# A decoder block on one core: the product of the convolution's two halves moves behind the low part of a later pair's second weights

## The chip, the cores and the metric

The kernel runs on one core of a Trainium2 chip. The metric is the time of one execution on the device in microseconds (us), as the median of several runs. The core has five engines that work side by side, each through an instruction queue of its own in the order in which the program was written out for it: TensorE (PE; its loading of weights is shown as PEld), VectorE (DVE), ScalarE (ACT), GpSimd (POOL) and SyncE (SP), which here only issues DMAs. An engine waits for another one at semaphores.

## The reference, cut to what matters

One decoder layer on 1024 positions of width 1024: gated linear attention and sparse attention side by side, then a gated feed-forward part with a short convolution, then a gated extra input, each followed by a layer norm. All is float32. The part that the change touches is this one, with `w_up` of 1024 x 5632 and `w_down` of 2816 x 1024:

```python
h = causal_dwconv(x @ w_up[i], conv_w[i], conv_b[i])
h_gate, h_val = jnp.split(h, 2, axis=-1)
ffn = (jax.nn.silu(h_gate) * h_val) @ w_down[i]
```

`causal_dwconv` gives each of the 5632 columns three weights over positions: `out[t] = w[2]*h[t] + w[1]*h[t-1] + w[0]*h[t-2] + b`.

## The kernel before, in words

**Products in parts.** TensorE multiplies in float32r. Each float32 operand is split into a high part (a cast, `hi_of`, L101) and a low part, what the cast lost (a subtraction, `lo_of`, L106), and a product is three matmuls: high by high, high by low, low by high (`mm3`). In the up stage the high part is cast on ScalarE ("wh" in the profile, written from the raw weights "wr" or "ar") and the low part ("wl") is made on GpSimd.

**Seven products for eight.** The up product x @ w_up goes through Strassen's scheme in Winograd's form. A column pair f (`up(f)`, 22 of them) is one block of 128 gate columns and one of 128 value columns. Its weights are four quarters of two raw tiles; four sums on VectorE (`left_operands`, the sums through L164, in place) make from them the seven left operands W0 to W6. In the order of the code: W0, first sum (a11 - a21), W5, second sum (a21 + a22, the profile's "ar<-ar" or "wr<-wr" with one input tile named), third sum (a22 - a11), W1, W2, W3, W4, fourth sum (a12 - a22), W6. A sum that overwrites a quarter has to wait until the parts made of it have been read: the fourth sum waits for W4's low part. The seven products p0 to p6 are 12 matmuls of 128x512 each, 84 for a pair, into PSUM banks "ch".

**From the products to the activation.** The results are added to two tiles "h" (value half and gate half, 128x1024) by VectorE (`plus`, L1043, one input a PSUM bank) and ScalarE (L1050 behind p0, L1074 behind p4). `conv(i)` then scales a half by the third convolution weight and adds the bias on ScalarE (L1085), adds the two shifted terms on VectorE (L1087, two instructions of 128x1023 and 128x1022, both inputs in SBUF), and, for the gate half, takes Silu on ScalarE (L1089), all in a tile "cv". In the stage's steady part `conv(1)` is the value half and `conv(0)` the gate half. GpSimd multiplies the two halves (L164 POOL, "cv<-cv,cv", L1096 calls it), and SP stores the product into `d_act` (L1097), from which the down stage reads it. "cv" has three buffers: the value half's tile is freed by the product, the gate half's by the store.

**What sets the order.** The code of pair f writes out W of pair f, then p0, p1, the late p6 of pair f-1, p5, `conv0` of f-1 (with the product and the store), p2, p3, p4 and `conv1` (the loop `for f in range(NF)`). A scheduler with a timeline of its own then reorders each engine's instructions before the program is built, so that the order on an engine isn't that of the code; an edge set by `tc.issue_after(x)` makes the instructions of a block come after x on x's engine. What each engine does in which order is fixed in the program.

Of the kernel before, what the change touches and what calls it, by code (L numbers as in the profile page):

```python
# [40 lines left out]
def hybrid_block(ctx: ExitStack, tc: tile.TileContext, x, p, w_in, w_gate_up, b_gate, g_gla, w_gla,  # L41
                 g_ckv, w_uv, w_dsa, w_out, ln1_g, ln1_b, w_up, conv_w, conv_b, w_down, ln2_g, ln2_b,
                 w_ple, w_ple_gate, ln3_g, ln3_b, out, tap=None):
    nc = tc.nc
    V, S, G, T = nc.vector, nc.scalar, nc.gpsimd, nc.tensor
# [9 lines left out]
    def pool(name, bufs=1, space=bass.MemoryType.SB, stack=ctx, **kw):  # L55
        return stack.enter_context(tc.tile_pool(name=name, bufs=bufs, space=space, reuse_waits="tile", **kw))
# [9 lines left out]
    def psum_banks(stack, tag, **kw):  # L66
        for name, bufs in kw.items():
            PS[name] = pool(f"ps_{tag}_{name}", bufs, PSUM, stack)
# [21 lines left out]
    def nm(s):  # L90
        uid[0] += 1
        return f"{s}_{uid[0]}"

    def bank(kind="mm", shape=(P, HALF)):
        return PS[kind].tile(list(shape), F32, name=nm(kind), tag=kind)

    done = {}

    def hi_of(dst, src, eng, scale=1.0):
        if eng == "A":  # L100
            S.activation(dst, src, AF.Copy, scale=scale)  # L101
        else:
            (V if eng == "V" else G).tensor_scalar(dst, src, scale, 0.0, ALU.mult, ALU.add)  # L103

    def lo_of(dst, src, hi, eng):
        done["GV"[eng != "G"]] = (G if eng == "G" else V).tensor_tensor(out=dst, in0=src, in1=hi.bitcast(F32), op=ALU.subtract)  # L106

    def split(hi, lo, src, eh="A", el="V"):
        hi_of(hi, src, eh)
        lo_of(lo, src, hi, el)  # L110
# [46 lines left out]
    def mm3(ps, l, r, start, stop, more=False):  # L157

        mm(ps, l[0], r[0], start, False, more)
        mm(ps, l[0], r[1], False, False, more)  # L160
        mm(ps, l[1], r[0], False, stop, more)

    def sums(out, a, b, op, eng="V"):
        (G if eng == "G" else V).tensor_tensor(out=out, in0=a, in1=b, op=op)  # L164

    def left_operands(a11, a12, a21, a22, put, e="VVVV"):

        return [lambda: put(0, a11),
                lambda: sums(a11, a11, a21, ALU.subtract, e[0]),
                lambda: put(5, a22),
                lambda: sums(a21, a21, a22, ALU.add, e[1]),
                lambda: sums(a22, a22, a11, ALU.subtract, e[2]),
                lambda: put(1, a22),
                lambda: put(2, a21),
                lambda: put(3, a11),
                lambda: put(4, a12),
                lambda: sums(a12, a12, a22, ALU.subtract, e[3]),  # L180
                lambda: put(6, a12)]
# [33 lines left out]
    def quad(a):  # L215
        return a.rearrange("p (a b) -> p a b", b=P)
# [39 lines left out]
    def run(steps):  # L256
        for f in steps:
            f()
# [16 lines left out]
    d_act = [dp.tile([P, 6, L], F32, name=f"d_act{c}") for c in range(4)]  # L275
# [47 lines left out]
    with ExitStack() as mix:  # L323
# [65 lines left out]
        with ExitStack() as c1:  # L389
# [95 lines left out]
            raw = wp.tile([P, 1024], F32, name=nm("wr"), tag="wr", bufs=2)  # L485
# [512 lines left out]
    with ExitStack() as c1:  # L998
        psum_banks(c1, "d", ch=8)
        fp = pool("ffwork", stack=c1)  # L1000
        rawp = pool("raws", stack=segd, side="right")
        wk = pool("upwork", stack=segk, side="right")
        UE, UE0, US = 'GGGGGGG', 'VVGVVGV', 'VVVV'
        nset = [0]

        def blocks(f):

            return (NF + f, f) if f < NF - 1 else (f, NF + f)

        def w_sets(f):  # L1010
            raw = []
            for c in blocks(f):
                if f % 2:
                    raw.append(rawp.tile([P, 6, 256], F32, name=nm("ar"), tag="ar", bufs=3)
                               .rearrange("p a b -> p (a b)")[:, :1024])
                else:
                    raw.append(wp.tile([P, 1024], F32, name=nm("wr"), tag="wr", bufs=2))
                nc.sync.dma_start(raw[-1].rearrange("p (k c) -> p k c", k=KT), wup_v[:, :, c * P:(c + 1) * P])
            W = []
            for _ in range(7):  # L1020
                n = nset[0] % 7
                nset[0] += 1
                pl, nb = (wq, 4) if n < 4 else (fp, 3)
                W.append([pl.tile([P, 512], F32R, name=nm(x), tag=x, bufs=nb) for x in ("wh", "wl")])
            run(left_operands(raw[1][:, :512], raw[1][:, 512:], raw[0][:, :512], raw[0][:, 512:],
                              lambda j, src: split(*W[j], src, "A", (UE if f else UE0)[j]), US))
            return [[quad(t) for t in w] for w in W]

        def up(f):

            W = w_sets(f)
            st, out_ = {}, {}

            def prod(ps, j, start):
                for k in range(4):
                    mm3(ps, (W[j][0][:, k], W[j][1][:, k]), (XS[j][:, 0, k], XS[j][:, 1, k]), start and k == 0, k == 3,
                        not start)  # L1040

            def plus(out, a, b):
                V.tensor_tensor(out=out, in0=a, in1=quad(b), op=ALU.add)  # L1043

            def p0():
                st["A"] = bank("ch")
                prod(st["A"], 0, True)
                st["h"] = [wk.tile([P, L], F32, name=nm("h"), tag=f"h{i}", bufs=2) for i in range(2)]
                st["hv"] = [h.rearrange("p (a g q) -> p g a q", g=2, q=P) for h in st["h"]]
                S.activation(st["hv"][1][:, 0], quad(st["A"]), AF.Copy)  # L1050

            def p1():
                st["B"] = bank("ch")
                prod(st["B"], 1, True)
                plus(st["hv"][0][:, 1], st["hv"][1][:, 0], st["B"])

            def p5():
                st["C"] = bank("ch")
                prod(st["C"], 5, True)

            def p2():
                st["D"] = bank("ch")
                prod(st["D"], 2, True)

            def p3():
                prod(st["B"], 3, False)
                s1, u3 = st["hv"][1][:, 0], st["hv"][1][:, 1]
                plus(u3, s1, st["B"])
                plus(s1, u3, st["C"])
                plus(u3, u3, st["D"])  # L1070

            def p4():
                prod(st["A"], 4, False)
                S.activation(st["hv"][0][:, 0], quad(st["A"]), AF.Copy)  # L1074

            def p6():
                prod(st["D"], 6, False)
                o = st["hv"][0][:, 1]
                plus(o, o, st["D"])

            def conv(i):
                c = blocks(f)[1 - i]
                h = st["h"][i]
                o = out_[c // NF] = wk.tile([P, L], F32, name=nm("cv"), tag="cv", bufs=3)
                S.activation(o, h, AF.Identity, bias=cbias[:, c:c + 1], scale=cw[:, 2, c:c + 1])  # L1085
                for d in (1, 2):
                    V.scalar_tensor_tensor(o[:, d:], h[:, :L - d], cw[:, 2 - d, c:c + 1], o[:, d:], ALU.mult, ALU.add)  # L1087
                if c < NF:
                    S.activation(o, o, AF.Silu)  # L1089

            def conv1():
                conv(1)

            def conv0():
                conv(0)
                sums(out_[0], out_[0], out_[1], ALU.mult, "G")  # L1096
                nc.sync.dma_start(d_act[f // 6][:, f % 6], out_[0])  # L1097
            return p0, p1, p5, p2, p3, p4, conv1, p6, conv0

        late = []  # L1100
        for f in range(NF):
            p0, p1, p5, p2, p3, p4, conv1, *rest = up(f)
            run([p0, p1, *late[:1], p5, *late[1:], p2, p3, p4, conv1])
            late = rest
        late[0]()
        last_conv = late[1]
    segx.close()
    sega.close()

# [7 lines left out]
    with ExitStack() as c1:  # L1117
# [88 lines left out]
            merge(*([wd_sets(c, cb)] if gi == 0 else []), *([act_sets(c, gi)] if cb == 0 else []))  # L1206
        prepare(*todo[0])
        with tc.issue_after(done["V"].ins):
            last_conv()
        segk.close()  # L1210
        open_residual(d_x1, 1, "right")
        res_all = RS["pool"].tile([P, NT, D], F32, name="res_all")
# [156 lines left out]
```

## Time and profile before

| | us |
|---|---|
| median of 3 runs | 2147.39 (2147.14 to 2148.36) |
| the profiled execution | 2145.27 |
| its span, first to last instruction | 2143.6 |
| between the two | 1.67 |

In the profile's rows the start is in us from the span's start, then come the duration, the engine, the line of the kernel, the operation, the tile written and the tiles read, and how many instructions are merged in the row (x4). What stands in brackets is how long the engine sat idle before it, and what ended that. The up stage lies between about 1305 and 1740 us; the down stage's first products follow.

### The profile page before, as it was taken

What the parts mean: (1) busy time and instruction counts of PE and PEld (TensorE: products, weight loads), DVE (VectorE), ACT (ScalarE), POOL (GpSimd) and SP (SyncE); (2) the same over time, 40 slices, a digit from 0 to 9 for tenths busy, and PEclk for the clock granted to TensorE, in tenths of its full rate; (3) what the DMA queues carried; (4) which work ended last, traced back from release to release, by engine and by line L of the source; (5) the groups of instructions that cost most, each with busy time, mean ns of one, the idle gap of its engine ahead of it and who ended that gap; (6) DMA issues with size and microseconds to landing.
All of it is one profiled execution on the core that took longest, in us unless ns stands there. A gap on an engine that the chain in (4) does not pass through costs nothing.

```text
span 2143.6 us, 32563 instructions
## 1 busy us (share of the span) xinstructions
PE 2063.3 (96%) x12210; PEld 1811.3 (84%) x12210; DVE 1564.6 (73%) x2742; ACT 846.0 (39%) x1540; POOL 1000.0 (47%) x832
## 2 busy tenths in 40 slices
PE   9999999999999999999999978999999979999997
PEld 8888899998988888887788976877777769989897
DVE  3589999999227888876234487777777788895965
ACT  4343312213126766675222244344344353342421
POOL 2423444535422121213231586776776684554753
PEclk9999999999999999999999998999999989999999
DMA  4322211211226686779766442222222134323222
GB/s 138 79 64 79 86 31 57 57 50 52 64 86 130 130 157 130 144 158 212 205 216 122 147 153 87 86 72 87 81 69 89 64 109 148 118 94 119 89 99 79
DMA packets 377566, 227.14 MB, mean 106 GB/s; under 512 B 189328, under 2 KB 351760, under 8 KB 377408
## 3 DMA queue, kind: packets, MB, share of 16 engines
q1 hardware_dynamic: 377408, 225.06, 38.7%
q8 instruction: 96, 1.57, 0.3%
q14 instruction: 62, 0.51, 0.1%
HBM read 146.37 MB, written 40.89 MB: 87 GB/s over the span
## 4 chain that ended last, share of the span: by engine, by line
PE 29%; DVE 9%; POOL 7%; issue 5%; DMA 3%; ACT 2%; SPq 0%; POOLq 0%; DVEq 0%; ACTq 0%
PE ch L155 16%; PE mm L155 13%; POOL wl L106 4%; DVE cv L1087 1%; DMA wr<-d_ob 1%; DVE cx L164 1%; DMA dr<-in_w_down_dram 1%; DVE h L1043 1%; ACT cv L1085 1%; DVE ar L164 1%; DVE wu L106 1%; DVE res_all L910 1%; DVE res_all L164 0%; DVE stats L933 0%; POOL lnmv L212 0%
## 5 line engine op out<-in xcount | busy, mean ns | idle before, releaser
L106 POOL TENSOR_TENSOR wl<-wr,wh 128x512 fp32r<-128x512 f32 x304 | 439.8, 1461 | 288.3 <-ACT wh L101 280.7
L155 PE MATMUL ch<-xs,wh 128*128 128x512 f32 x1232 | 384.8, 394 | 5.8 <-ACT wh L101 3.2
L155 PE MATMUL mm<-Ah,wh 128*128 128x512 f32 x832 | 332.1, 399 | 2.7 <-ACT wh L101 1.6
L155 PE MATMUL mm<-Al,wh 128*128 128x512 f32 x832 | 330.4, 397 | 0.3 <-POOL Al L106 0.3
L155 PE MATMUL mm<-Ah,wl 128*128 128x512 f32 x832 | 329.4, 396 | 0.0
L155 PEld LDWEIGHTS ch<-xs,wh 128*128 128x128 f32 x1232 | 231.5, 189 | 58.7 <-DVE h L1043 4.1
L103 POOL TENSOR_SCALAR wh<-wr 128x512 fp32r<-128x512 f32 x112 | 75.2, 674 | 381.1 <-PE mm L155 194.4
L155 PE MATMUL ch<-xs,wl 128*128 128x512 f32 x616 | 242.8, 395 | 6.8 <-POOL wl L106 6.7
L155 PE MATMUL mm<-wl,Ah 128*128 128x256 f32 x768 | 217.1, 284 | 5.2 <-POOL wl L106 5.1
L155 PE MATMUL mm<-wh,Al 128*128 128x256 f32 x768 | 215.8, 283 | 0.0
L155 PE MATMUL ch<-wu,au 128*128 128x256 f32 x1512 | 194.0, 292 | 22.5 <-DVE au L106 7.2
L155 PE MATMUL mm<-wh,Ah 128*128 128x256 f32 x768 | 213.2, 283 | 0.0
L1087 DVE SCALAR_TENSOR_TENSOR cv<-h,cw,cv 128x1023 f32<-128x1023 f32 x88 | 168.6, 1915 | 60.0 <-ACT cv L1085 58.5
L155 PEld LDWEIGHTS ch<-wu,au 128*128 128x128 f32 x1512 | 190.4, 199 | 25.9 <-DVE au L106 8.1
L101 ACT ACTIVATE wh<-wr 128x512 fp32r<-128x512 f32 (+1 forms) x201 | 120.5, 623 | 194.7 <-PE mm L155 81.6
L155 PEld LDWEIGHTS mm<-Ah,wh 128*128 128x128 f32 x832 | 156.7, 188 | 33.4 <-ACT wh L101 2.1
L155 PEld LDWEIGHTS mm<-Ah,wl 128*128 128x128 f32 x832 | 156.4, 188 | 33.0
L155 PEld LDWEIGHTS mm<-Al,wh 128*128 128x128 f32 x832 | 156.5, 188 | 30.7 <-POOL Al L106 0.8
L674 DVE MATCH_REPLACE8 score<-m,score 128x896 f32<-128x896 f32 (+3 forms) x192 | 166.5, 869 | 0.0
L673 DVE MAX8 m<-score 128x8 f32<-128x896 f32 (+3 forms) x192 | 163.6, 876 | 2.3 <-POOL score L480 2.1
L155 PEld LDWEIGHTS mm<-wl,Ah 128*128 128x128 f32 x768 | 145.1, 189 | 7.1 <-POOL wl L106 6.4
L155 PEld LDWEIGHTS ch<-xs,wl 128*128 128x128 f32 x616 | 116.5, 189 | 38.2 <-POOL wl L106 14.0
(269 smaller groups left out, 4328.4 us busy)
## 6 DMA issues: line engine op xcount, KB each, us to landing
wr<-in_w_in_dram SPq DMA_DIRECT2D x60, 512.0 KB, 3.8
wr<-in_w_up_dram SPq DMA_DIRECT2D x22, 512.0 KB, 3.9
ar<-in_w_up_dram SPq DMA_DIRECT2D x22, 512.0 KB, 4.0
d_act<-cv SPq DMA_DIRECT2D x22, 512.0 KB, 2.6
dr<-in_w_down_dram SPq DMA_DIRECT2D x12, 768.0 KB, 7.0
ar<-d_act SPq DMA_DIRECT2D x12, 768.0 KB, 5.1
d_tg<-tg SPq DMA_DIRECT2D x32, 256.0 KB, 2.0
wr<-in_w_out_dram SPq DMA_DIRECT2D x16, 512.0 KB, 3.6
```

The costliest lines, as they stand in the source:

```text
L101: S.activation(dst, src, AF.Copy, scale=scale)
L103: (V if eng == "V" else G).tensor_scalar(dst, src, scale, 0.0, ALU.mult, ALU.add)
L106: done["GV"[eng != "G"]] = (G if eng == "G" else V).tensor_tensor(out=dst, in0=src, in1=hi.bitcast(F32), op=ALU.subtract)
L155: T.matmul(ps, lhsT=l, rhs=r, start=start, stop=stop, skip_group_check=more)
L164: (G if eng == "G" else V).tensor_tensor(out=out, in0=a, in1=b, op=op)
L673: V.max(m8, score[t])
L674: V.match_replace(score[t], m8, score[t], TAKEN)
L910: V.scalar_tensor_tensor(r[:, a:b], r[:, a:b], mv[:, 2:3], gb[1][:, a:b], ALU.mult, ALU.add)
L1043: V.tensor_tensor(out=out, in0=a, in1=quad(b), op=ALU.add)
L1085: S.activation(o, h, AF.Identity, bias=cbias[:, c:c + 1], scale=cw[:, 2, c:c + 1])
L1087: V.scalar_tensor_tensor(o[:, d:], h[:, :L - d], cw[:, 2 - d, c:c + 1], o[:, d:], ALU.mult, ALU.add)
```

## The change

The product and its store leave `conv0` and become a step of their own, `store`. Pair f - 2's store is written out in turn f, after the weights of pair f, and has to come after the instruction that `done["G"]` held when W1 of pair f was split, which is W1's low part on GpSimd (for f > 1). The last two stores follow the loop and `last_conv`.

```diff
-            run(left_operands(raw[1][:, :512], raw[1][:, 512:], raw[0][:, :512], raw[0][:, 512:],
-                              lambda j, src: split(*W[j], src, "A", (UE if f else UE0)[j]), US))
+            def put(j, src):
+                split(*W[j], src, "A", (UE if f else UE0)[j])
+                if j == 1 and f:
+                    second[0] = done["G"]
+            run(left_operands(raw[1][:, :512], raw[1][:, 512:], raw[0][:, :512], raw[0][:, 512:], put, US))
...
             def conv0():
                 conv(0)
+
+            def store():
                 sums(out_[0], out_[0], out_[1], ALU.mult, "G")
-                nc.sync.dma_start(d_act[f // 6][:, f % 6], out_[0])
-            return p0, p1, p5, p2, p3, p4, conv1, p6, conv0
-
-        late = []
+                sent[0] = nc.sync.dma_start(d_act[f // 6][:, f % 6], out_[0])
+            return p0, p1, p5, p2, p3, p4, conv1, p6, conv0, store
+
+        late, stores, sent = [], [], [None]
         for f in range(NF):
-            p0, p1, p5, p2, p3, p4, conv1, *rest = up(f)
+            p0, p1, p5, p2, p3, p4, conv1, *rest, store = up(f)
+            if f > 1:
+                with tc.issue_after(second[0].ins):
+                    stores.pop(0)()
+            stores.append(store)
             run([p0, p1, *late[:1], p5, *late[1:], p2, p3, p4, conv1])
             late = rest
+        stores[0]()
         late[0]()
-        last_conv = late[1]
+        last_conv = [late[1], stores[1]]
...
-            last_conv()
+            run(last_conv)
```

What the scheduler made of it differs on three engines; ScalarE's and SP's orders are the same as before. The pair shown is the thirteenth (f = 12); tile numbers differ by two or so between the programs. On GpSimd, before, in the middle of the up stage: these are the low parts of W0 of pair 12, W6 of pair 11 and W5 of pair 12, the product of pair 10, and the low parts of W1, W2 and W3 of pair 12.

```order
L106 TENSOR_TENSOR wl_14755<-wr_14752,wh_14754 128x512
L106 TENSOR_TENSOR wl_14623<-ar_14608,wh_14622 128x512
L106 TENSOR_TENSOR wl_14765<-wr_14750,wh_14764 128x512
L164 TENSOR_TENSOR cv_14698<-cv_14698,cv_14602 128x1024
L106 TENSOR_TENSOR wl_14757<-wr_14750,wh_14756 128x512
L106 TENSOR_TENSOR wl_14759<-wr_14750,wh_14758 128x512
L106 TENSOR_TENSOR wl_14761<-wr_14752,wh_14760 128x512
```

The same place on GpSimd in the changed kernel, where W1's low part is `wl_14755`:

```order
L106 TENSOR_TENSOR wl_14753<-wr_14750,wh_14752 128x512
L106 TENSOR_TENSOR wl_14621<-ar_14606,wh_14620 128x512
L106 TENSOR_TENSOR wl_14763<-wr_14748,wh_14762 128x512
L106 TENSOR_TENSOR wl_14755<-wr_14748,wh_14754 128x512
L164 TENSOR_TENSOR cv_14698<-cv_14698,cv_14600 128x1024
L106 TENSOR_TENSOR wl_14757<-wr_14748,wh_14756 128x512
L106 TENSOR_TENSOR wl_14759<-wr_14750,wh_14758 128x512
```

The product has gone one place back, behind W1; this holds for twenty pairs, and nothing else moves on GpSimd. On VectorE, before, at the place where the fourth sum of pair 11 has just run: the first and second sums of pair 12, the first add to h of pair 11, the last add to h of pair 10, and that half's convolution.

```order
L164 TENSOR_TENSOR wr_14752<-wr_14752,wr_14750 128x512
L164 TENSOR_TENSOR wr_14750<-wr_14750 128x512
L1043 TENSOR_TENSOR h_14655<-h_14656,ch_14658 128x4x128
L1043 TENSOR_TENSOR h_14511<-h_14511,ch_14561 128x4x128
L1087 SCALAR_TENSOR_TENSOR cv_14698<-h_14511,cw,cv_14698 128x1023
```

The same place on VectorE in the changed kernel (the lines of the adds and of the convolution are three higher there):

```order
L164 TENSOR_TENSOR wr_14750<-wr_14750,wr_14748 128x512
L1046 TENSOR_TENSOR h_14655<-h_14656,ch_14658 128x4x128
L164 TENSOR_TENSOR wr_14748<-wr_14748 128x512
L1046 TENSOR_TENSOR h_14511<-h_14511,ch_14559 128x4x128
L1090 SCALAR_TENSOR_TENSOR cv_14698<-h_14511,cw,cv_14698 128x1023
```

The first add to h and the second sum have changed places; so it is in 17 pairs in a row, and in the pair ahead of them the add stands even before the first sum. On TensorE the scheduler had interleaved matmuls of p1, p6 and p5 (two of p1, four of p5, one of p6, the rest of p1, of p6 and of p5); in the changed kernel p1, p6 and p5 follow each other whole. The number of instructions is the same on every engine.

More of the change, by code (lines that the diff above doesn't have):

```diff
@@ L1003, in hybrid_block @@
         UE, UE0, US = 'GGGGGGG', 'VVGVVGV', 'VVVV'
-        nset = [0]
+        nset, second = [0], [None]
         def blocks(f):
```

## The prediction

> **What bounds the kernel now.** The forecast is slower, 2168.7 us against 2147.39 us. The change touches the stage of the up product (22 column pairs, from about 1305 us to 1740 us), so I first read how long the run is, and then how TensorE fares in two stretches of that stage, each about one column pair long. The first line is the head of the page; the other two are busy time by engine (PE, PEld, DVE, ACT, POOL with the number of instructions, then the granted clock).
>
> ```profile
> span 2143.6 us, 32563 instructions
> ```
>
> ```profile
> 1342.00:1361.00 19.00, 19.00 (x85) 15.75 (x84) 13.72 (x13) 8.25 (x13) 13.21 (x9) 1.00 0.23 71
> 1460.00:1480.00 20.00, 19.45 (x84) 15.61 (x84) 14.68 (x14) 8.37 (x14) 14.22 (x10) 1.00 0.26 82
> ```
>
> TensorE looks like the bound, and early in the stage it is: a pair has 84 matmuls, and 85 run in 19.00 us without a gap. Later it needs 20 us for 84. What sets that slower pace is seen in ScalarE's timeline: L1050 copies a pair's first product out, L1089 is the Silu that ends the convolution of a pair's gate half, once per pair.
>
> ```profile
> 1336.02 1.06 ACT L1089 ACTIVATE cv<-cv 128x1024 f32<-128x1024 f32 x1
> ...
> 1342.12 0.58 ACT L1050 ACTIVATE h<-ch 128x512 f32<-128x512 f32 x1
> ...
> 1361.16 0.58 ACT L1050 ACTIVATE h<-ch 128x512 f32<-128x512 f32 x1
> ...
> 1713.97 1.06 ACT L1089 ACTIVATE cv<-cv 128x1024 f32<-128x1024 f32 x1 [3.12 <-DVE cv L1087]
> ```
>
> TensorE alone needs 1361.16 - 1342.12 = 19.04 us for a pair. From the first Silu to the twentieth it is (1713.97 - 1336.02) / 19 = 19.89 us. So TensorE has 0.85 us to spare in each pair and something else paces it. Here is one pair in the timeline of all engines; TensorE's rows are left out but the one that waits.
>
> ```profile
> 1495.02 1.06 ACT L1089 ACTIVATE cv<-cv 128x1024 f32<-128x1024 f32 x1 [3.11 <-DVE cv L1087]
> 1495.45 2.12 DVE L1043 TENSOR_TENSOR h<-h,ch 128x512 f32<-128x512 f32 x3
> 1495.99 1.66 ACT L101 ACTIVATE wh<-wr 128x512 fp32r<-128x512 f32 x3
> 1496.22 2.42 POOL L164 TENSOR_TENSOR cv<-cv,cv 128x1024 f32<-128x1024 f32 x1 [2.37 <-issue]
> ...
> 1498.58 7.00 POOL L106 TENSOR_TENSOR wl<-wr,wh 128x512 fp32r<-128x512 f32 x4
> 1498.89 4.30 DVE L1087 SCALAR_TENSOR_TENSOR cv<-h,cw,cv 128x1023 f32<-128x1023 f32 x2 [1.32 <-ACT cv L1085]
> ...
> 1499.93 0.50 PE L155 MATMUL ch<-xs,wl 128*128 128x512 f32 x1 [0.39 <-POOL wl L106]
> ...
> 1505.54 1.28 POOL L106 TENSOR_TENSOR wl<-ar,wh 128x512 fp32r<-128x512 f32 x1
> 1505.61 1.75 DVE L164 TENSOR_TENSOR wr<-wr,wr 128x512 f32<-128x512 f32 x1 [2.43 <-POOL wl L106]
> ...
> 1507.46 0.63 ACT L101 ACTIVATE wh<-wr 128x512 fp32r<-128x512 f32 x1 [6.60 <-DVE wr L164]
> 1508.00 0.69 DVE L164 TENSOR_TENSOR ar<-ar 128x512 f32<-128x512 f32 x1
> 1508.17 1.68 POOL L106 TENSOR_TENSOR wl<-wr,wh 128x512 fp32r<-128x512 f32 x1 [1.35 <-ACT wh L101]
> 1508.61 1.28 DVE L1043 TENSOR_TENSOR h<-h,ch 128x512 f32<-128x512 f32 x2
> ...
> 1510.01 1.24 ACT L1085 ACTIVATE cv<-h,cbias,cw 128x1024 f32<-128x1024 f32 x1 [1.91 <-DVE h L1043]
> ...
> 1511.28 3.51 DVE L1087 SCALAR_TENSOR_TENSOR cv<-h,cw,cv 128x1023 f32<-128x1023 f32 x2 [1.39 <-ACT cv L1085]
> ...
> 1514.88 1.06 ACT L1089 ACTIVATE cv<-cv 128x1024 f32<-128x1024 f32 x1 [3.11 <-DVE cv L1087]
> ```
>
> This is a closed ring. From Silu to product 1.20 us; the product, to W1, 2.36; the low parts of W1 to W4, to W0, 6.96; VectorE's fourth sum, which may overwrite its tile only when W4 has been read, 0.07 later; from there to the second sum 2.39; to the two adds of h 0.61; to the scaling by the convolution's weight 1.40; to the two convolution operations 1.27; to the next Silu 3.60. Sum 19.86 us, the measured period, and every step starts when the one before ends. TensorE isn't a link: it feeds h long before it is used, and stalls (0.39 us at W1) because the ring is slower than its 19.04 us. A change pays only if it shortens the ring.
>
> **Part one: the product behind W1.** Nothing is added or removed; twenty times the product changes places with the low part of W1 on GpSimd. In the ring of before, the product starts 1.20 us after the Silu starts (1496.22 - 1495.02). W1 can't start then: its high part is cast on ScalarE, whose order is unchanged, behind the Silu. The cast starts 0.97 us after the Silu (1495.99), and a cast needs 0.71 us until its low part starts (1507.46 to 1508.17). So GpSimd goes on 0.97 + 0.71 = 1.68 us after the Silu starts, 0.48 us later than now. The product no longer waits for anything but W1, yet it still stands between the Silu and W4: the ring goes through Silu, cast, W1, product, W2, W3, W4.
>
> The length of this row is 2.36 + 6.96 = 9.32 us now. Alone, a low part takes 1.28 us (row 1505.54), so 6.96 - 4 x 1.28 = 1.84 us of it is waiting for VectorE's two convolution operations (1498.89), which then come between the product and W2, W3. Should they fall elsewhere and free GpSimd by up to 1.84 us, nothing is won, since they stand ahead of the fourth sum on VectorE and it would wait for them; should a turn be lost, it is some tenths. I take 9.32 unchanged, within 0.15 us a pair. Price: 0.48 us for each of the 19 steps from Silu to Silu, 9.1 us.
>
> W1 itself is ready 1.68 + 1.28 = 2.96 us after the Silu, where TensorE now waits until 4.91 us after it (1499.93). That stall is relieved against the ring but doesn't pay: TensorE will wait for the later ring, about 19.04 against 21.07 us. Its own order changes too, with p1, p6 and p5 now whole instead of interleaved; that costs nothing while it has two microseconds to spare.
>
> **The store.** It follows the product on SP. It is issued some 1.7 us later against the Silu (W1 and 0.48), and the weight loads queued behind it wait for the fourth sum, seven microseconds after that, as they do now. The tile that it frees is wanted a whole pair later. Cost nothing.
>
> **Part two: one add before the second sum.** In 18 of these 19 steps VectorE now does the first add of h (L1043) before the sum "ar<-ar" instead of after it. Two rows, each with least, median and greatest duration in ns, tell what that does beside GpSimd:
>
> ```profile
> L164 POOL TENSOR_TENSOR cv<-cv,cv x22: 2402/2411/2702, 1337.2 to 1767.1; 128x1024 f32<-128x1024 f32 x22
> ```
>
> ```profile
> L1043 DVE TENSOR_TENSOR h<-h,ch x110: 673/682/690, 1309.9 to 1737.8; 128x512 f32<-128x512 f32 x110
> ```
>
> The adds of h read a bank of PSUM; they run beside the product (1495.45 and 1496.22) and neither gets longer. The sums of L164 have both inputs in SBUF, and they exclude GpSimd: the fourth sum, issued at 1505.61 while W0 ran from 1505.54 to 1506.82, took 1.75 us instead of 0.69 and ended 0.54 us behind W0; and W6, issued at 1508.17 while the second sum ran, took 1.68 us instead of 1.28. In before the second sum starts first (1508.00) and W6 waits, which costs the ring nothing. Now at 1508.17 VectorE is in an add that doesn't hinder GpSimd: W6 starts at once and holds until 1509.45. The second sum, due at 1508.61, then ends at 1509.45 + 0.54 = 1509.99, and the last add 0.60 us later (half of 1.28 and less the overlap), at 1510.59. Now the two adds end at 1508.61 + 1.28 = 1509.89. The scaling on ScalarE, and all behind it, comes 0.70 us later: 18 x 0.70 = 12.6 us. If the sum did win the port, it would be zero; I take 0.70, by the fourth sum's row, which is the same operation behind the same instruction on GpSimd.
>
> The Trainium skill (SBUF — State Buffer, section "Who interferes with whom") says that a VectorE instruction with two SBUF inputs and a GpSimd instruction that reads SBUF exclude each other for a whole instruction, and that the first to issue goes first. The trace agrees on the order. By the page the loser blocks fully, so that the sum's whole 0.69 us would follow W6, not 0.54: by it 18 x 0.15 = 2.7 us more, 2171.4 us. The measured 0.54 is used.
>
> **The end of the stage.** The ring's lateness has to arrive. After the last Silu of the ring the chain of waits goes this way:
>
> ```profile
> 1717.53 1.31 POOL wl L106
> 1718.88 12.33 PE ch L155 x53
> 1731.23 0.70 DVE h L1043
> ```
>
> W1 of the last pair will be there 1.9 us sooner after that Silu, but five more matmuls are left behind it (58 instead of 53, by 0.23 us 1.2 us): up to 0.8 us back. VectorE ahead of that h is itself 0.48 us late. I take 0.4 us back.
>
> **Sum.** 9.1 + 12.6 - 0.4 = 21.3 us. The profiled execution took 2145.27 us (span 2143.6 and 1.67 around it) and would take 2166.6; it lies 2.1 us under the median of the runs, and on the median the forecast is 2147.39 + 21.3 = 2168.7 us.
>
> **The rivals.**
> - The order on VectorE costs nothing (the sum takes the port after all, or W6 comes later than I think). For it: the two meet within half a microsecond. Against it: row 1505.61. Then only part one is left: 9.1 - 0.4, 2156.1 us.
> - Faster: TensorE's wait for W1 is the link that paces the stage, and the ring follows it. Then, with W1 two microseconds sooner, the period falls to 19.04 us, 19 x 0.85 = 16 us off, 2131.2 us. For it: the chain of waits passes several times from W1 to TensorE, and a wait of 0.39 us is in every pair. Against it: the ring adds up to the period without TensorE. It decides if VectorE's fourth sum no longer waits on W4.
> - No change to speak of: the product does move by only one place, and the convolution operations, meeting the product instead of W2, give back what the hop costs, with the order on VectorE harmless: 2147 us, give or take 4.
> - Worse: the later product throws out more turns of the port, say another low part (1.28 us) in half of the pairs: 10 x 1.28, 2181.5 us. No row shows such a loss.
>
> **How the numbers follow.** Forecast 0.62, harmless order 0.16, faster 0.07, no change 0.08, worse 0.07. The range takes the forecast with its unknowns (0.15 us a pair either way is 2.9 us; the 2.7 us above) up to 2175, and the first rival with 2.9 us less on the other side, 2153: from 2153 to 2175 us. A measurement of this kernel tells about 0.2% (4.3 us) from no change. Faster by more than that 0.07, within it 0.08, slower 0.85.
>
> **What would show it.** The Silus some 21.07 us apart, not 19.89; GpSimd idle about 2.85 us ahead of W1 instead of 2.37 ahead of the product; the product straight behind W1 without a wait; the sum "ar<-ar" at 1.3 us instead of 0.69 and W6 at 1.28 instead of 1.68; TensorE idle some two microseconds in a pair, before W1 and before p3. Silus 20.4 us apart mean the first rival; a period near 19 us, with TensorE never waiting, means that the ring was no ring and I am wrong.

## The result and the profile after

| | before | after |
|---|---|---|
| median of the runs, us | 2147.44 (2147.14 to 2148.36) | 2170.03 (2167.93 to 2170.91) |
| ratio, 95% interval | | 1.0103 (1.0086 to 1.0121) |
| the profiled execution, us | 2145.27 | 2170.65 |

The change makes the kernel 22.6 us slower. The two stretches of about one pair, in the changed kernel:

```profile
1342.00:1361.00 19.00, 19.00 (x85) 15.76 (x84) 14.32 (x13) 6.75 (x10) 11.65 (x8) 1.00 0.27 83
1460.00:1480.00 20.00, 18.88 (x81) 14.70 (x80) 15.12 (x13) 7.35 (x11) 13.67 (x8) 1.00 0.21 66
```

At first TensorE runs as it did; later 81 matmuls fit into 20 us instead of 84, at a full clock (1.00). The Silus on ScalarE, L1092 there, the first, two in the middle and the twentieth:

```profile
1336.45 1.06 ACT L1092 ACTIVATE cv<-cv 128x1024 f32<-128x1024 f32 x1
...
1505.04 1.06 ACT L1092 ACTIVATE cv<-cv 128x1024 f32<-128x1024 f32 x1 [3.12 <-DVE cv L1090]
...
1526.05 1.06 ACT L1092 ACTIVATE cv<-cv 128x1024 f32<-128x1024 f32 x1 [3.12 <-DVE cv L1090]
...
1736.63 1.06 ACT L1092 ACTIVATE cv<-cv 128x1024 f32<-128x1024 f32 x1 [3.12 <-DVE cv L1090]
```

(1736.63 - 1336.45) / 19 = 21.06 us from Silu to Silu, where it was 19.89: over 19 steps 400.18 - 377.95 = 22.2 us. Nearly the whole loss is there. Between these two Silus the timeline has the ring again (TensorE's rows, and rows of the other engines that lie beside the ring, are left out):

```profile
1506.01 1.66 ACT L101 ACTIVATE wh<-wr 128x512 fp32r<-128x512 f32 x3
1506.70 1.28 POOL L106 TENSOR_TENSOR wl<-wr,wh 128x512 fp32r<-128x512 f32 x1 [2.83 <-ACT wh L101]
...
1507.94 2.40 POOL L164 TENSOR_TENSOR cv<-cv,cv 128x1024 f32<-128x1024 f32 x1
...
1508.90 4.75 DVE L1090 SCALAR_TENSOR_TENSOR cv<-h,cw,cv 128x1023 f32<-128x1023 f32 x2 [1.31 <-ACT cv L1088]
...
1510.30 5.74 POOL L106 TENSOR_TENSOR wl<-wr,wh 128x512 fp32r<-128x512 f32 x3
...
1516.00 1.28 POOL L106 TENSOR_TENSOR wl<-ar,wh 128x512 fp32r<-128x512 f32 x1
1516.08 1.75 DVE L164 TENSOR_TENSOR wr<-wr,wr 128x512 f32<-128x512 f32 x1 [2.43 <-POOL wl L106]
...
1517.75 0.68 DVE L164 TENSOR_TENSOR ar<-ar,ar 128x512 f32<-128x512 f32 x1
...
1518.36 0.67 DVE L1046 TENSOR_TENSOR h<-h,ch 128x512 f32<-128x512 f32 x1
1518.63 1.28 POOL L106 TENSOR_TENSOR wl<-wr,wh 128x512 fp32r<-128x512 f32 x1 [1.35 <-ACT wh L101]
1518.95 1.50 DVE L164 TENSOR_TENSOR ar<-ar 128x512 f32<-128x512 f32 x1
1520.38 0.68 DVE L1046 TENSOR_TENSOR h<-h,ch 128x512 f32<-128x512 f32 x1
1521.17 1.25 ACT L1088 ACTIVATE cv<-h,cbias,cw 128x1024 f32<-128x1024 f32 x1 [2.62 <-DVE h L1046]
...
1522.45 3.51 DVE L1090 SCALAR_TENSOR_TENSOR cv<-h,cw,cv 128x1023 f32<-128x1023 f32 x2 [1.40 <-ACT cv L1088]
```

Two places show the two prices. GpSimd waits 2.83 us for the cast of W1 and starts 1.66 us after the Silu (1506.70), where the product started 1.20 us after it; the product then follows W1 without a wait, and from W1 to W0 it is 9.30 us as before (9.32). And the second sum takes 1.50 us, since it was issued beside W6 (1518.63 to 1519.91) and ended 0.54 us behind it; W6 has its plain 1.28 us. From the fourth sum to the scaling it is 5.09 us, formerly 4.40. From the scaling to the convolution operations it is 1.28 us and from there to the next Silu 3.60, as before; the steps add up to 21.01 us.

TensorE now waits twice in a pair, before p3 for the add to h and in p1 for W1 and its cast. Before, the wait ahead of p3 held up only its weight load (0.26 us at 1509.35). The rows after:

```profile
1508.03 0.50 PE L155 MATMUL ch<-xs,wl 128*128 128x512 f32 x1 [0.62 <-POOL wl L106]
...
1519.08 0.74 PE L155 MATMUL ch<-xs,wh 128*128 128x512 f32 x2 [0.32 <-DVE h L1046]
```

### The profile page after: what moved, and what is told of

Read it like the earlier page. It is cut to its first block, busy times and chain, and to the rows that moved or that the text cites. A ratio compares the mean times of both kernels' runs of the same rounds, so it can differ in the third digit from the quotient of the medians.

```text
span 2168.9 us, 32578 instructions
## 1 busy us (share of the span) xinstructions
PE 2071.6 (96%) x12210; PEld 1809.4 (83%) x12210; DVE 1593.1 (73%) x2742; ACT 846.2 (39%) x1540; POOL 991.2 (46%) x832
## 4 chain that ended last, share of the span: by engine, by line
PE 19%; POOL 11%; DVE 10%; issue 9%; DMA 3%; ACT 2%; SPq 0%; POOLq 0%; DVEq 0%; ACTq 0%
PE mm L155 14%; POOL wl L106 7%; PE ch L155 5%; DVE ar L164 2%; POOL cv L164 1%; DVE h L1046 1%; DVE cx L164 1%; DVE wr L164 1%; DMA dr<-in_w_down_dram 1%; DMA wr<-d_ob 1%; ACT wh L101 1%; DVE au L106 1%; DVE res_all L164 1%; DVE wu L106 1%; DVE um L164 1%
## 5 line engine op out<-in xcount | busy, mean ns | idle before, releaser
L106 POOL TENSOR_TENSOR wl<-wr,wh 128x512 fp32r<-128x512 f32 x304 | 435.1, 1444 | 328.4 <-ACT wh L101 318.9
L155 PE MATMUL ch<-xs,wl 128*128 128x512 f32 x616 | 242.5, 394 | 11.3 <-POOL wl L106 11.3
L1090 DVE SCALAR_TENSOR_TENSOR cv<-h,cw,cv 128x1023 f32<-128x1023 f32 x88 | 177.8, 2021 | 59.9 <-ACT cv L1088 58.4
L106 POOL TENSOR_TENSOR wl<-ar,wh 128x512 fp32r<-128x512 f32 x77 | 123.8, 1620 | 84.4 <-ACT wh L101 83.0
```

The costliest lines, as they stand in the source:

```text
L155: T.matmul(ps, lhsT=l, rhs=r, start=start, stop=stop, skip_group_check=more)
```

## The experiments

Six kernels, each timed against the kernel before on the same chip in three rounds. Each prediction and each reading below is for the steps from Silu to Silu as well, since the runs of one kernel differ by 2 to 6 us. The kernel before had a median of 2145.9 us in both of these sessions.

**VectorE's order alone.** The kernel before, with an edge that puts the second sum behind the first add to h:

```diff
-            run(left_operands(..., US))
+            steps = left_operands(..., US)
+            run(steps[:3])
+            with tc.issue_after(first[0].ins) if 1 < f < NF - 1 else ExitStack():
+                steps[3]()
+            run(steps[4:])
```

Here `first[0]` is the add of p1. GpSimd's, ScalarE's, TensorE's and SP's orders are those of before. In the program the order is changed in 19 pairs; 18 of them lie between the first and the twentieth Silu. In the one ahead of them the second sum kept its plain 0.68 us (1328.64).

> The kernel before with one part of the change alone: on VectorE the second sum stands behind the first add to h in 18 pairs; every other engine's order is that of before. Theory of the ring: W6 takes the shared port, the sum waits 0.7 us, the ring is 20.6 us in 18 steps: 18 x 0.70 = 12.6 us, 2160 us (2157 to 2163), Silus 20.6 us apart, the sum at 1.5 us instead of 0.69. Rival, the order on VectorE is harmless: 2147.4 us. Rival, TensorE's wait for W1 paces: W1 comes no sooner, and the first add earlier frees p3: 2147 us or 5 less.

Measured: 2161.06 us, ratio 1.0070 (1.0055 to 1.0085). In VectorE's timeline, at the second sum:

```profile
1513.97 0.67 DVE L1047 TENSOR_TENSOR h<-h,ch 128x512 f32<-128x512 f32 x1
1514.56 1.53 DVE L164 TENSOR_TENSOR ar<-ar 128x512 f32<-128x512 f32 x1
```

and in GpSimd's, W6:

```profile
1514.25 1.30 POOL L106 TENSOR_TENSOR wl<-wr,wh 128x512 fp32r<-128x512 f32 x1 [1.35 <-ACT wh L101]
```

The sum waits for W6 as in the changed kernel, without any move of the product. The Silus are 20.56 us apart on average (first 1336.42, twentieth 1727.09), 20.60 in the middle: 12.7 us over 19 steps, 12.6 expected. The rival that this order is harmless falls, and so does the one that TensorE's wait for W1 paces, which allowed no loss. The median moved 15 us, 2.4 more than the steps.

**The product's move alone.** The changed kernel, with an edge that holds the first add to h behind the second sum again:

```diff
+            if 1 < f < NF - 1:
+                tc.add_manual_dep(first[0].ins, done["S"].ins.name, NOSYNC, reason="order")
```

It stands right behind the second sum in `w_sets`; `done["S"]` is that sum, and NOSYNC stands here for the argument (shortened) that makes the edge one of order, without a wait. GpSimd's, ScalarE's, TensorE's and SP's orders are those of the changed kernel. In one pair, the last but one, the order of the change remained.

> The changed kernel with the first add to h put back behind the second sum: what is left of the change is the product behind W1 on GpSimd and TensorE's order. Theory of the ring: only the hop from Silu to W1 is left, 19 x 0.48 = 9.1 less 0.4: 2156 us (2153 to 2159), Silus 20.37 us apart. Rival, the move of the product costs all of it and VectorE's order nothing: 2170 us. Rival, the order on VectorE costs all: 2147 us. Rival, TensorE's wait for W1 paces: W1 is 2 us sooner, 2131 us.

Measured: 2158.42 us, ratio 1.0058 (1.0043 to 1.0073). Two Silus in the middle, and the first of GpSimd's rows between them:

```profile
1498.18 1.06 ACT L1098 ACTIVATE cv<-cv 128x1024 f32<-128x1024 f32 x1 [3.13 <-DVE cv L1096]
...
1518.54 1.06 ACT L1098 ACTIVATE cv<-cv 128x1024 f32<-128x1024 f32 x1 [3.12 <-DVE cv L1096]
```

```profile
1499.84 1.30 POOL L106 TENSOR_TENSOR wl<-wr,wh 128x512 fp32r<-128x512 f32 x1 [2.84 <-ACT wh L101]
1501.10 2.41 POOL L164 TENSOR_TENSOR cv<-cv,cv 128x1024 f32<-128x1024 f32 x1
```

A step is 20.36 us, 20.37 expected, and the second sum is back at 0.69 us. From the first to the twentieth Silu it is 387.69 us (1335.37 to 1723.06), 9.7 us more than before, of which 0.7 belongs to the one pair with the other order. The median moved 12.5 us, 2.8 more than the steps. W1 came 2 us sooner against the Silu and the kernel got slower: TensorE's wait for W1 isn't what paces the stage.

**The last add first.** The kernel before, with two edges on VectorE. The last add of pair f-1, behind p6, goes ahead of the fourth sum of pair f and of the first sum of pair f+1; in the order that results, the fourth, first and second sums stand between that add and its convolution operations, where VectorE waited for ScalarE's scaling. The first add goes ahead of the three sums with it. With these edges the scheduler also changed two other orders: on ScalarE the scaling stands ahead of W6's cast, and TensorE interleaves p1, p6 and p5 in another way.

```diff
+                add = sixth[0] = plus(o, o, st["D"])
+                if 0 < f < NF - 2:
+                    tc.add_manual_dep(fourth[0].ins, add.ins.name, NOSYNC, reason="order")
...
+            with tc.issue_after(sixth[0].ins) if 1 < f < NF - 1 else ExitStack():
+                steps[1]()
```

> The kernel before, but on VectorE the last add to h of the pair before (and with it ScalarE's scaling) stands ahead of the fourth, first and second sums instead of behind them; GpSimd's order is as before. Theory of the ring: the two adds, and the wait for the scaling, leave the ring; 19.86 - 2.67 = 17.2 us is less than TensorE's 19.04, so TensorE paces: 18 x 0.85 = 15 us off, 2132 us (2129 to 2137), TensorE without a gap in the stage. Rival, something other than the ring (TensorE's wait for W1, the port's load) paces: 2147 us, since W1 and the port's work are the same.

Measured: 2134.44 us, ratio 0.9943 (0.9928 to 0.9957). The two stretches by engine:

```profile
1342.00:1361.00 19.00, 19.00 (x85) 15.76 (x84) 14.05 (x14) 8.51 (x13) 16.91 (x10) 1.00 0.32 108
1460.00:1480.00 20.00, 20.00 (x90) 16.57 (x89) 12.80 (x13) 8.38 (x12) 16.64 (x10) 1.00 0.25 79
```

TensorE runs without a gap, 90 matmuls in 20 us. The steps are 19.03 us (1487.97 to 1507.00). What GpSimd and VectorE have to do and W1's place are as before, so it was the ring that paced. The first step is 17.19 us (1337.49 to 1354.68), the length worked out for the ring, 17.2; but that is luck. In this step the fourth sum stands behind the last add, which waited for TensorE, and not for W4, as VectorE's rows show:

```profile
1348.55 0.69 DVE L1049 TENSOR_TENSOR h<-h,ch 128x512 f32<-128x512 f32 x1 [1.74 <-PE ch L155]
1349.15 0.69 DVE L164 TENSOR_TENSOR wr<-wr,wr 128x512 f32<-128x512 f32 x1
```

GpSimd's row for W0 at that place:

```profile
1347.95 1.29 POOL L106 TENSOR_TENSOR wl<-ar,wh 128x512 fp32r<-128x512 f32 x1
```

In the ring the sum would have been issued beside W0 and have ended 0.54 us behind it, at 1349.78; it came 1.1 us later, ran its plain 0.69 us and ended at 1349.84. TensorE's result and the ring's happened to arrive together, so this run shows that TensorE paces once the ring is short, and not how long the ring is. The median gained 11.5 us, not 15; what the record says of the difference is taken up below.

**The change with the last add first.** The same two edges in the changed kernel.

> The changed kernel with the same order on VectorE as in the run with the last add first: product behind W1, but the ring short. Theory of the ring: 17.2 + 0.48 = 17.7 us is still under TensorE's 19.04, so the product's place costs nothing: 2132 us, within 2 us of the other one. Rival, the product behind W1 costs by itself (by the port or by the later store): 9 us more than the other one.

Measured: 2134.40 us, ratio 0.9947 (0.9930 to 0.9963), the same as the one before. The product behind W1 costs nothing when the ring is short enough: what it costs, it costs through the ring; the later store, or GpSimd's and VectorE's load, has no price of its own. TensorE's order here is that of the changed kernel, with p1, p6 and p5 whole, and its pace is 19.03 us all the same (1485.37 to 1504.40). The first four steps, before TensorE paces, were 18.71 us (1335.79 to 1354.50 the first) and not the 17.7 expected; VectorE's convolution operations show why:

```profile
1386.68 0.69 DVE L164 TENSOR_TENSOR ar<-ar 128x512 f32<-128x512 f32 x1
1387.29 4.55 DVE L1100 SCALAR_TENSOR_TENSOR cv<-h,cw,cv 128x1023 f32<-128x1023 f32 x2
```

They took 4.55 us instead of 3.51, 1.04 more, with both W6 and W5 beside them, as GpSimd's rows have it:

```profile
1386.85 1.67 POOL L106 TENSOR_TENSOR wl<-wr,wh 128x512 fp32r<-128x512 f32 x1 [1.35 <-ACT wh L101]
1388.48 2.28 POOL L106 TENSOR_TENSOR wl<-ar,wh 128x512 fp32r<-128x512 f32 x1
```

So the ring did grow by more than the hop, by another microsecond of turns between GpSimd and VectorE, and it stayed hidden only because 18.71 is still under 19.04.

**Without the product.** The kernel before, without GpSimd's product; the gate half alone is stored. The up stage's order on VectorE is unchanged; TensorE's there is that of the changed kernel.

```diff
             def conv0():
                 conv(0)
-                sums(out_[0], out_[0], out_[1], ALU.mult, "G")
                 nc.sync.dma_start(d_act[f // 6][:, f % 6], out_[0])
```

> The kernel before without the product on GpSimd: the gate half alone is stored, so the activation isn't that of the reference; VectorE's order in the up stage is that of before, TensorE's that of the changed kernel, and a few instructions of the down stage change places. Theory of the ring: Silu, cast, W1 to W4 and on is 19.86 - 2.36 + 0.48 = 17.98 us, under TensorE's 19.04, so TensorE paces: Silus 19.04 us apart, about 15 us off, 2131 to 2135 us with what the down stage does. Rival, the port's or GpSimd's load paces: 2.4 us less in each pair, Silus 17.5 us apart or TensorE at its 19.04 as well. Rival, the product was hidden: 2146 us, Silus 19.89 us apart.

Measured: 2133.18 us, ratio 0.9937 (0.9923 to 0.9952). The first steps are 17.98 and 17.99 us (Silus at 1335.82, 1353.80 and 1371.79), the ring's 17.98 to the hundredth. The first of them goes link by link as the sum has it: W1 1.66 us after the Silu (1337.48), W0 6.97 later (1344.45), then the fourth sum, which waited for W4:

```profile
1344.53 1.77 DVE L164 TENSOR_TENSOR wr<-wr,wr 128x512 f32<-128x512 f32 x1 [1.18 <-POOL wl L106]
1346.22 0.68 DVE L164 TENSOR_TENSOR ar<-ar,ar 128x512 f32<-128x512 f32 x1
1346.93 0.69 DVE L164 TENSOR_TENSOR ar<-ar 128x512 f32<-128x512 f32 x1
1347.54 1.28 DVE L1043 TENSOR_TENSOR h<-h,ch 128x512 f32<-128x512 f32 x2
```

In the second the fourth sum (1362.51) already follows VectorE's convolution operations without a wait for W4, so only the first is evidence for the chain. From then on TensorE paces, 19.04 us (1466.96 to 1486.00). The product was in the ring with its 2.36 us, less the hop to W1's cast. The median gained 12.7 us, and no other place of the product can be expected to gain much more, since here there is none and TensorE paces; that is argued, not shown.

**The product behind W3.** The run of the product's move alone, with `j == 3` for `j == 1`: the product stands behind W3, one place ahead of W4.

> Like the run with the product's move alone (VectorE's order as before), but the product behind the low part of W3 instead of W1, one place ahead of W4. Theory of the ring: from the Silu to W4 there are the same instructions after the same cast, in another order; 20.36 us from Silu to Silu again, 2156 us, within 2 us of that run. Rival, what costs is that the product meets the two convolution operations at the port: now W2 and W3 meet them as in before, and the step is back at 19.9 us, 2147 us.

Measured: 2157.24 us, ratio 1.0046 (1.0029 to 1.0063). Two Silus lie 20.35 us apart (1500.63 to 1520.98), so the rival with 19.9 falls. The median moved 11.3 us, and from the first to the twentieth Silu it is 9.3 us more than before (1337.87 to 1725.13). GpSimd, from W1 to W0:

```profile
1502.29 4.79 POOL L106 TENSOR_TENSOR wl<-wr,wh 128x512 fp32r<-128x512 f32 x3 [2.83 <-ACT wh L101]
1507.03 3.38 POOL L164 TENSOR_TENSOR cv<-cv,cv 128x1024 f32<-128x1024 f32 x1
1510.37 1.29 POOL L106 TENSOR_TENSOR wl<-wr,wh 128x512 fp32r<-128x512 f32 x1
1511.61 1.30 POOL L106 TENSOR_TENSOR wl<-ar,wh 128x512 fp32r<-128x512 f32 x1
```

The product itself now takes 3.38 us, since it meets a convolution operation, and W1 to W3 take less; from W1 to W0 it is 9.32 us again. The three orders of these five instructions that were tried take the same time; only what has to come before the first of them differs, a Silu (1.20 us) or a Silu and a cast (1.66).

## Why the prediction was right

- **The ring.** Shown. The two runs that shorten it (last add first, no product) fall to TensorE's 19.04 us a pair and no further. The first step without the product gives the ring's own length as the sum had it, 17.98 us, link by link; the 17.19 us of the other run agree by luck.
- **The hop from Silu to W1's cast**, 0.48 us a step: alone it made 20.36 instead of 19.89, which is 0.47. That the row of product and four low parts keeps its length (9.32, within 0.15) held in all orders tried: 9.30 to 9.34.
- **The order on VectorE**, 0.70 us a step: alone it made 20.60 us, 0.71. The measured 0.54 us behind W6 was the right figure for the sum: 1518.63 + 1.28 + 0.54 is 1520.45, and the sum ended at 1518.95 + 1.50 = 1520.45. By the rule of the Trainium skill (SBUF — State Buffer, section "Who interferes with whom"), that the other instruction is blocked for the whole of the first, the prediction had put the sum's full 0.69 us behind W6 into its upper bound; the measurement decides for 0.54. The same section of the Trainium skill says that the first to issue goes first and that a VectorE instruction with one SBUF input doesn't contend with GpSimd. The trace of after agrees: the sum issued after W6 ends behind it, and the add with an input in PSUM (1518.36) and W6 (1518.63) overlap and keep their 0.67 and 1.28 us.
- **The number of steps** was one too low. The prediction counts 18 of the 19 steps with the new order on VectorE, but it stands in all of them: it is in 18 pairs in a row, not 17, behind the one in which the add stands even before the first sum. The last step of the changed kernel, 21.01 us (1715.62 to 1736.63), has it too:

```profile
1728.93 0.67 DVE L1046 TENSOR_TENSOR h<-h,ch 128x512 f32<-128x512 f32 x1
1729.53 1.50 DVE L164 TENSOR_TENSOR ar<-ar 128x512 f32<-128x512 f32 x1
```

So this term should have been 19 x 0.70 = 13.3 us and the sum 22.0; the median lost 22.6.
- **The two together** add up: 12.72 us over the 19 steps with VectorE's order alone and 9.74 with the product's move alone (where the last step has the new order as well) are 22.46, and the changed kernel has 22.23. The step with the add before the first sum was longer than the others, 21.32 us (1336.45 to 1357.77).
- **The end of the stage**, 0.4 us back: the down stage's first long run of matmuls starts 1787.24 - 1764.91 = 22.33 us later, while the first Silu was 0.43 later (over all runs it lies between 1335.37 and 1337.87) and the steps cost 22.23. So 0.33 came back.

The rows of TensorE on which this rests, before and then after:

```profile
1764.91 20.96 PE L155 MATMUL ch<-wu,au 128*128 128x256 f32 x160 [3.22 <-POOL au L106]
```

```profile
1787.24 21.87 PE L155 MATMUL ch<-wu,au 128*128 128x256 f32 x160 [3.23 <-POOL au L106]
```

- **TensorE's waits**: two in a pair, before W1 and before p3, as said, but the idle time shown is 0.62 + 0.32 us and now and then 0.15 for the cast, not two. The count of matmuls is the better measure: 81 in 20 us against 85 in 19.00 where nothing stalls. After each wait the next matmuls are shown longer (0.74 us for two), and that hides part of the stall. TensorE's own change of order was not run alone; the steps leave no room for a price of it, since the hop accounts for the run that has that order and VectorE's old one.

What the sum didn't hold is behind the stage. The profiled execution lost 25.4 us, the stage 22.3. The first 20 us of the down stage, before and after:

```profile
1764.90:1784.90 20.00, 19.99 (x154) 19.99 (x155) 17.92 (x28) 6.97 (x15) 11.71 (x9) 0.91 0.62 234
```

```profile
1787.20:1807.20 20.00, 19.96 (x146) 19.96 (x147) 18.54 (x28) 6.71 (x15) 11.21 (x8) 0.86 0.61 237
```

The granted clock is 0.86 instead of 0.91 there, and eight matmuls fewer fit in. The run with the last add first has 0.86 too in its first 20 us of the down stage; its stage ended 13.7 us earlier (first long run at 1751.21), its profiled execution gained 10.7, its median 11.5. With VectorE's order alone, the product's move alone and the product behind W3 the medians moved 2.0 to 2.8 us more than the steps, too; the kernel before had a median 1.5 us lower in those sessions, which may be part of it. Why the clock comes back later in some profiles wasn't tried, and neither was what makes up the rest of these 3 us; the runs of one kernel spread by as much (2167.93 to 2170.91).

## What to carry to other kernels

When the busiest engine idles a little in every turn of a loop, add up the steps on the other engines from one event to the same event a turn later: if they close to the period, that ring may be the bound, and a run with one link taken out tells whether it is. Moving a link to another place within the ring gains nothing. What helps is to take something out of it; here an add that stood behind three sums in VectorE's queue was worth 0.6% (ratio 0.9943), where the product's new place by itself cost 0.6% (1.0058) and the whole change 1%. And look at what a scheduler does elsewhere: more than half of this change's loss came from two instructions that the diff doesn't touch.

## What the runs showed of the hardware

Where a VectorE instruction with two inputs in SBUF met one of GpSimd, the two took turns so exactly that sums over rows came out to some hundredths of a microsecond. A VectorE sum of 0.69 us that was issued while GpSimd ran ended 0.54 us behind GpSimd's instruction (behind W0 and behind W6). A product of 2.40 us became 3.38 when a convolution operation was already running. The stretch from the first of the five GpSimd instructions to W0 took 9.30 to 9.34 us in the three orders tried: which instruction was delayed changed, the stretch didn't.
